# The bank of the gated rows' transposes in a mixture-of-experts block: from the two transpose banks to the six product banks

## The chip, the cores and the metric

The kernel runs on one core of one Trainium2 chip. The metric is the device time of one execution in microseconds (us); of several executions the median is taken.

## The reference, cut to what matters

A block of two layers works on 512 latent rows of 1024 numbers. Each layer has a token mixer and then a mixture of 32 SwiGLU experts, of which each row uses two; the change is in this second part, which runs once in each layer. Rows are sorted by expert and each expert's weights act on its own rows:

```
def expert_block(args):
    xi, e = args
    return (jax.nn.silu(xi @ w1[e]) * (xi @ w3[e])) @ w2[e]
...
y = jax.ops.segment_sum(yb * buf_w[:, None].astype(yb.dtype), buf_tok, num_segments=t + 1)
```

All 32 experts' weights are read in each layer, 6 MB an expert.

## The kernel before

**Pairs of experts.** The function `moe(l)` handles the experts of layer `l` in 16 pairs `p`. A pair has up to 64 rows for each of its two experts, side by side on 128 partitions; TensorE (PE) multiplies the two halves in two column halves of its array, with two sets of weights. A loop runs over pairs 0 to 14, and pair 15 is written out behind it. The whole function stands in a manual schedule: each engine gets its instructions in the order of the code.

**One pair on PE.** In order:

1. `gate_up` and `lin_up` (both line 1499): the rows times `w1` and times `w3`. ScalarE (ACT) takes the silu of the first, VectorE (DVE) multiplies the second with it (line 1508), which gives the gated rows `g`.
2. `scatter(*prev)` (lines 1562 and 1563): the rows of the pair before are added to their tokens by eight pairs of products with a selection matrix. DVE adds each of the eight results to `xs` (line 1564).
3. `turn_g(g)` (line 1514): four transposes of the gated rows into one bank `pg`, which ACT copies to `gT` (line 1516).
4. `turn` (line 1485): eight transposes of the next pair's input rows, four into each of two banks. DVE takes the first bank to `hT` with the modulation (line 1491), ACT the second (line 1489).
5. `down` (line 1526): `gT` times `w2` in two halves. DVE weighs them (line 1532), ACT and GpSimd split them for the next scatter.

**Banks.** PSUM, where PE writes, has eight banks; line 433 names them: two are `tr` (transposes) and six are `pj` (products). Each call of `bank` takes one of its kind that an earlier tile has used, and PE then waits until that tile's last reader is done with it.

**Branches.** An expert may have more than 64 rows. For that, three blocks under `tc.If(n > 64)` stand in each pair's code: behind `gate_up`, behind `lin_up`, and (lines 1644 to 1646) a whole `turn_g`, `down` and `scatter` between steps 2 and 3, which takes one `tr` and ten `pj` banks. The banks are laid out when the program is built, as if the blocks ran. In this execution two of the thirty blocks ran, and 28 were skipped. Where a block is skipped, each engine raises, in its place, the counts that the block would have raised, each after its own earlier work; whoever waits for a bank that the block used last waits for this raise. The same stands behind pair 15's scatter: a loop under an If (`rest`, line 1660) that was skipped in both layers.

**Weights.** They come in units of 2 MB into a ring of nine buffers, six units a pair, in the order in which they are used, through one DMA queue; a unit is asked for when its buffer comes free.

Of the kernel before, what the change touches and what calls it, by code (L numbers as in the profile page):

```python
# [34 lines left out]
class Net:  # L35
# [1424 lines left out]
    def moe(self, l):  # L1460
        tc, nc, I = self.tc, self.nc, self.I
        with ExitStack() as ms:
# [46 lines left out]

            def turn_g(g, gT=None):  # L1510

                pg = self.bank("tr")
                for k in range(4):
                    nc.tensor.transpose(pg[:, 128 * k:128 * k + 128], g[:, k::4], self.ident)  # L1514
                gT = wk.tile([128, 4, 128], F32, name="gT") if gT is None else gT[:, :512].rearrange("p (k d) -> p k d", k=4)
                nc.scalar.activation(gT, pg.rearrange("p (k d) -> p k d", k=4), AF.Copy)  # L1516
                return gT
# [67 lines left out]
            def block(p, c, g):  # L1585

                pool = self.rings["B"][0]
                ix = wk.tile([128, 1], I32, name="ix")
                iw = wk.tile([128, 2], F32, name="iw")
                nc.vector.tensor_copy(ix, self.gxc[:, bass.ds(c, 1)])  # L1590
                nc.vector.tensor_copy(iw[:, 0:1], self.tid[:, bass.ds(c, 1)])
                nc.vector.tensor_copy(iw[:, 1:2], self.wsl[:, bass.ds(c, 1)])
                hT = turn(gather(ix, hx[0]), hx[0])

                def unit(name, x):
                    w = pool.tile([128, 4096], F32, name="w")
                    nc.sync.dma_start(w, I[name][l, bass.ds(2 * p + x, 1)].rearrange("e (p k) n -> p (e k n)", p=128))
                    return w.rearrange("p (k n) -> p k n", n=1024 if name == "w2" else 512)
                gate_up(hT, (unit("w1", 0), unit("w1", 1)), g)
                lin_up(hT, (unit("w3", 0), unit("w3", 1)), g)  # L1600
                o = out()
                down(turn_g(g, hx[1]), (unit("w2", 0), unit("w2", 1)), iw[:, 0:1], iw[:, 1:2], o, g)
                scatter(*o)
# [20 lines left out]
            for p in range(15):  # L1624
                n = ns.pop(p)
                w = self.next_unit(), self.next_unit(1)
                g = wk.tile([128, 512], F32, name="g")
                gate_up(hT, w, g, () if p else (route, range(8)))
                with tc.If(n > 64):  # L1629

                    hTx = turn(hx[p % 2], hx[p % 2])
                    gate_up(hTx, w, gx)
                w = self.next_unit(), self.next_unit(1)
                lin_up(hT, w, g)
                with tc.If(n > 64):  # L1635
                    lin_up(hTx, w, gx)
                if p < 14:
                    hgs.append(gather(col(self.gix, p + 2), skip=True))
                    self.issue(self.taken)
                if prev:  # L1640
                    scatter(*prev)
                w = self.next_unit(), self.next_unit(1)
                prev = out()
                with tc.If(n > 64):
                    down(turn_g(gx, hx[p % 2]), w, col(self.tid, 16 + p), col(self.wsl, 16 + p), prev, gx)
                    scatter(*prev)
                gT = turn_g(g)
                hT = turn(hgs.pop(0))
                if p < 13:
                    ns[p + 2] = more(p + 2)  # L1650
                prev = out()
                down(gT, w, col(self.tid, p), col(self.wsl, p), prev, g, nc.gpsimd if p < 14 else nc.vector)
# [295 lines left out]
```

## Time and profile before

| | |
|---|---|
| median of 3 runs | 1859.27 us (1853.28 to 1860.14) |
| the profiled execution | 1858.2 us, its span 1856.1 us |
| mean granted clock of TensorE | 0.964 of 2.4 GHz |
| PE busy | 1682.1 us, 91% of the span |
| pairs of layer 0 | from about 620 us to about 1125 us |
| pairs of layer 1 | from about 1345 us to the end |

All times in the rows are us from the start of the span. PE rows are matmuls (a transpose is one), PEld rows the loads of the operand that stays in the array. "[1.97 <-DVEq L1660]" says that the engine sat idle for 1.97 us before the row, and what ended it; DVEq, PEq and SPq are the sequencers of these engines, which raise and wait for semaphores. A granted clock (PEclk) of 1.00 is 2.4 GHz and 0.50 is 1.2 GHz.

### The profile page before, as it was taken

To read this page: it belongs to the slowest core of one execution; us is meant where nothing else is said; L and a number is where in the kernel's file an instruction comes from. 1 tells how busy PE (TensorE), PEld (TensorE's weight loads), DVE (VectorE), ACT (ScalarE), POOL (GpSimd) and SP (SyncE) were. 2 spreads that over 40 slices of the span, in tenths; PEclk is the share of its full clock that TensorE was granted. 3 is DMA by queue.
4 is the path that set the end of the run, shared out by engine and by line. 5 is a ranking of instruction groups with operands and counts; after the bars stand their busy time and mean duration, and the time that the engine had idled before them with its cause. 6 is when DMAs were issued, how large, how long until landed. Compare 5 with 4: busy or idle time off the path is not lost. (4 is left out here: it accounts for less than half of the span.)

```text
span 1856.1 us, 26571 instructions
## 1 busy us (share of the span) xinstructions
PE 1682.1 (91%) x10229; PEld 1005.1 (54%) x10230; DVE 803.9 (43%) x1614; ACT 481.8 (26%) x888; POOL 419.4 (23%) x303
## 2 busy tenths in 40 slices
PE   5999988897989699999999998999789999999996
PEld 4766667766868244444344446688634444444442
DVE  5435778745773423323233237633523233323233
ACT  4466354522322111111111115233311111111012
POOL 1114465644510111011111103343111111111101
PEclk9999989998999799999999998999999999999998
DMA  9569985769944899999999864714589979999993
GB/s 328 199 231 338 283 224 171 173 162 257 228 163 158 343 424 427 425 424 426 425 425 424 367 257 148 278 45 181 227 320 425 427 294 427 426 424 426 426 425 150
DMA packets 154547, 572.27 MB, mean 308 GB/s; under 512 B 55208, under 2 KB 79961, under 8 KB 126214
## 3 DMA queue, kind: packets, MB, share of 16 engines
q1 hardware_dynamic: 148326, 555.26, 78.6%
q0 software_dynamic: 4896, 10.48, 1.5%
q10 hardware_dynamic: 1152, 4.19, 0.6%
q8 instruction: 112, 1.84, 0.4%
q14 instruction: 61, 0.50, 0.1%
HBM read 550.86 MB, written 26.38 MB: 311 GB/s over the span
## 5 line engine op out<-in xcount | busy, mean ns | idle before, releaser
L1499 PE MATMUL pj<-w,hT 128*64 128x512 f32 x2048 | 470.1, 597 | 16.8 <-DMA w<-in_w 10.4
L1499 PEld LDWEIGHTS pj<-w,hT 128*64 128x64 f32 x2048 | 171.1, 137 | 295.6 <-issue 259.5
L1526 PE MATMUL pj<-w,gT 128*64 128x512 f32 x960 | 212.6, 595 | 3.8 <-DVE hT L1491 2.6
L1537 POOL TENSOR_TENSOR ylo<-g,yhi 128x512 fp32r<-128x512 f32 x56 | 70.8, 1264 | 642.0 <-ACT yhi L1536 642.0
L1508 DVE TENSOR_TENSOR g<-pj,g 128x512 f32<-128x512 f32 x32 | 22.1, 692 | 435.7 <-PEq L1635 383.5
L1564 DVE TENSOR_TENSOR xs<-pj,xs 128x512 f32<-128x512 f32 x264 | 161.4, 681 | 4.7 <-PE pj L1563 0.9
L670 POOL TENSOR_TENSOR wlo<-w,whi 128x1024 fp32r<-128x1024 f32 x43 | 107.0, 2492 | 231.2 <-ACT whi L668 229.7
L1526 PEld LDWEIGHTS pj<-w,gT 128*64 128x64 f32 x960 | 77.2, 137 | 118.2 <-issue 111.9
L1532 DVE SCALAR_TENSOR_TENSOR g<-pj,wsl,gate 128x512 f32<-128x512 f32 x64 | 48.1, 751 | 174.4 <-PE pj L1526 154.2
L1516 ACT ACTIVATE gT<-tr 128x512 f32<-128x512 f32 x32 | 19.1, 597 | 371.7 <-PE tr L1514 371.7
L1562 PE MATMUL pj<-yhi,sel 128*128 128x512 f32 x264 | 106.7, 404 | 5.6 <-PEq L1635 2.4
L685 PE MATMUL pj<-w,whi 128*128 128x512 f32 x336 | 104.9, 392 | 0.6 <-ACT whi L668 0.6
L1563 PE MATMUL pj<-ylo,sel 128*128 128x512 f32 x264 | 103.5, 392 | 1.4 <-POOL ylo L1537 1.4
L685 PE MATMUL pj<-hhi,wlo 128*128 128x512 f32 x224 | 93.5, 417 | 10.0 <-POOL wlo L670 7.0
L685 PE MATMUL pj<-hhi,whi 128*128 128x512 f32 x224 | 93.1, 416 | 7.2 <-DVE cv L801 6.3
L685 PE MATMUL pj<-hlo,whi 128*128 128x512 f32 x224 | 91.2, 407 | 0.0
L1536 ACT ACTIVATE yhi<-g 128x512 fp32r<-128x512 f32 x62 | 39.0, 629 | 192.7 <-DVE g L1532 192.7
L1562 PEld LDWEIGHTS pj<-yhi,sel 128*128 128x128 f32 x264 | 49.5, 187 | 45.8 <-issue 32.5
L685 PEld LDWEIGHTS pj<-w,whi 128*128 128x128 f32 x336 | 63.6, 190 | 15.0 <-ACT whi L668 1.0
L668 ACT ACTIVATE whi<-w 128x1024 fp32r<-128x1024 f32 x53 | 55.2, 1052 | 55.8 <-PE pj L685 37.6
L1505 ACT ACTIVATE g<-pj 128x512 f32<-128x512 f32 x32 | 19.1, 597 | 185.4 <-PEq L1629 144.4
L685 PE MATMUL pj<-w,wlo 128*128 128x512 f32 x168 | 66.3, 394 | 0.0
(623 smaller groups left out, 2722.2 us busy)
## 6 DMA issues: line engine op xcount, KB each, us to landing
w<-in_w SPq DMA_DIRECT2D x188, 2048.0 KB
w<-in_ada_w SPq DMA_DIRECT2D x20, 2048.0 KB
w<-in_w_in_a SPq DMA_DIRECT2D x8, 2048.0 KB
w<-in_w_in_b SPq DMA_DIRECT2D x6, 2048.0 KB
w<-in_ada_w SPq DMA_DIRECT2D x8, 1024.0 KB
w<-in_w SPq DMA_DIRECT2D x8, 1024.0 KB
Y<-R SPq DMA_DIRECT2D x20, 256.0 KB
vp<-vscr SPq DMA_DIRECT2D x18, 256.0 KB
```

Of the source, the lines that this page charges most:

```text
L668: nc.scalar.activation(hi[:, :, :n], w, AF.Copy)
L670: (lo_eng or nc.gpsimd).tensor_tensor(lo[:, :, :n], w, hi[:, :, :n].bitcast(F32), op=OP.subtract)
L685: nc.tensor.matmul(out, n[j][0][:, k], n[j][1][:, k, a:b], start=(i == 0), stop=(i == 23))
L1499: nc.tensor.matmul(ps[64 * x:64 * x + 64], hT[:, k, 64 * x:64 * x + 64], w[x][:, k], start=(k == 0), stop=(k == 7))
L1508: nc.vector.tensor_tensor(g, up(hT, w, side), g, op=OP.mult)
L1526: nc.tensor.matmul(py[64 * x:64 * x + 64], gT[:, k, 64 * x:64 * x + 64], w[x][:, k, 512 * n:512 * n + 512], start=(k == 0), stop=(k == 3))
L1532: nc.vector.scalar_tensor_tensor(y, py, wi, self.gate[:, 512 * n:512 * n + 512], op0=OP.mult, op1=OP.mult)
L1536: nc.scalar.activation(o[0][:, c], y, AF.Copy)
L1537: eng.tensor_tensor(o[1][:, c], y, o[0][:, c].bitcast(F32), op=OP.subtract)
L1562: nc.tensor.matmul(ps, s, yhi[:, c], start=True, stop=False)
L1563: nc.tensor.matmul(ps, s, ylo[:, c], start=False, stop=True)
L1564: nc.vector.tensor_tensor(self.xs[:, t, c], ps, self.xs[:, t, c], op=OP.add)
```

## The change

`turn_g` takes its bank from the six of the products. Nothing else is edited. The call in the If block (line 1645) and the one in `rest` go through the same function, so they move too.

```
             def turn_g(g, gT=None):

-                pg = self.bank("tr")
+                pg = self.bank("pj")
                 for k in range(4):
                     nc.tensor.transpose(pg[:, 128 * k:128 * k + 128], g[:, k::4], self.ident)
                 gT = wk.tile([128, 4, 128], F32, name="gT") if gT is None else gT[:, :512].rearrange("p (k d) -> p k d", k=4)
```

## Rows read from the trace of the kernel before

**Rows 1.** The page: busy time, share and count of each engine.

```profile
PE 1682.1 (91%) x10229; PEld 1005.1 (54%) x10230; DVE 803.9 (43%) x1614; ACT 481.8 (26%) x888; POOL 419.4 (23%) x303
```

**Rows 2.** Busy time by stretches: start:end, length, engines, PEclk, DMA share, GB/s.

```profile
839.00:980.00 141.00, 129.80 (x573) 55.36 (x572) 40.64 (x75) 19.19 (x39) 18.64 (x16) 1.00 1.01 426
...
1706.00:1828.00 122.00, 113.03 (x501) 51.69 (x502) 38.57 (x70) 15.82 (x32) 9.58 (x8) 0.99 0.96 401
```

**Rows 3.** Timeline of one pair, layer 0, pair 2: start, length, engine, line.

```profile
697.03 4.87 DVE L1564 TENSOR_TENSOR xs<-pj,xs 128x512 f32<-128x512 f32 x8
...
699.74 0.39 PE L1563 MATMUL pj<-ylo,sel 128*128 128x512 f32 x1
700.25 0.56 PEld L1514 LDWEIGHTS tr<-ident,g 128*128 128x128 f32 x4 [0.54 <-issue]
...
700.72 0.54 PEld L1485 LDWEIGHTS tr<-ident,hg 128*128 128x128 f32 x4
...
701.04 0.60 ACT L1516 ACTIVATE gT<-tr 128x512 f32<-128x512 f32 x1 [11.50 <-PE tr L1514]
701.68 0.52 PEld L1485 LDWEIGHTS tr<-ident,hg 128*128 128x128 f32 x4 [0.43 <-ACT gT L1516]
...
702.05 1.37 DVE L1491 TENSOR_SCALAR hT<-tr,m 128x128 f32<-128x128 f32 x4 [0.15 <-DVEq L1644]
...
702.53 0.23 PEld L1526 LDWEIGHTS pj<-w,gT 128*64 128x64 f32 x4 [0.32 <-DVE hT L1491]
```

**Rows 4.** Instructions by line: who waited for line 1516 (us, times).

```profile
  PEld tr L1485: 13.0, 30
```

**Rows 5.** By line: line 1514's engine sat idle until (us, times).

```profile
  DVEq L1660: 3.9, 2
```

**Rows 6.** By line: the events of line 1644 on DVE's sequencer.

```profile
L1644 DVEq EVENT_SEMAPHORE x28: 21/21/21, 645.3 to 1797.8; - x28
```

**Rows 7.** Timeline of PE: starts of `turn_g` in both layers.

```profile
672.70 0.72 PE L1514 MATMUL tr<-ident,g 128*128 128x128 f32 x4
...
839.41 0.72 PE L1514 MATMUL tr<-ident,g 128*128 128x128 f32 x4
...
963.67 0.72 PE L1514 MATMUL tr<-ident,g 128*128 128x128 f32 x4
...
1074.74 0.72 PE L1514 MATMUL tr<-ident,g 128*128 128x128 f32 x4
...
1103.44 0.72 PE L1514 MATMUL tr<-ident,g 128*128 128x128 f32 x4 [1.97 <-DVEq L1660]
...
1540.09 0.72 PE L1514 MATMUL tr<-ident,g 128*128 128x128 f32 x4
...
1705.85 0.72 PE L1514 MATMUL tr<-ident,g 128*128 128x128 f32 x4 [0.15 <-PEq L1644]
...
1796.13 0.72 PE L1514 MATMUL tr<-ident,g 128*128 128x128 f32 x4 [0.15 <-PEq L1644]
...
1827.24 0.72 PE L1514 MATMUL tr<-ident,g 128*128 128x128 f32 x4 [1.90 <-DVEq L1660]
```

**Rows 8.** Stretches around long waits of PE, columns as in rows 2.

```profile
855.00:870.00 15.00, 12.68 (x52) 4.83 (x49) 2.22 (x4) 0.60 (x1) 0.00 (x0) 1.00 1.00 422
945.00:962.00 17.00, 14.39 (x61) 5.38 (x57) 2.26 (x4) 0.60 (x1) 0.03 (x1) 1.00 1.01 427
...
1725.00:1735.00 10.00, 9.37 (x33) 3.14 (x34) 0.63 (x1) 0.00 (x0) 0.00 (x0) 0.83 1.01 430
...
1098.00:1115.00 17.00, 15.03 (x56) 7.08 (x56) 7.04 (x12) 3.52 (x6) 0.00 (x0) 0.90 0.73 256
1822.00:1840.00 18.00, 16.11 (x59) 7.12 (x57) 6.97 (x12) 2.71 (x4) 0.00 (x0) 0.91 0.09 36
```

**Rows 9.** Timeline of PE: thirty matmuls of `lin_up` behind waits for weights.

```profile
860.44 7.08 PE L1499 MATMUL pj<-w,hT 128*64 128x512 f32 x30 [2.02 <-DMA w<-in_w]
...
1725.47 8.78 PE L1499 MATMUL pj<-w,hT 128*64 128x512 f32 x30 [1.71 <-DMA w<-in_w]
```

More of the change, by code (lines that the diff above doesn't have):

```diff
@@ L1510, in turn_g @@
             def turn_g(g, gT=None):
-                pg = self.bank("tr")
+                pg = self.bank("pj")
                 for k in range(4):
```

## The prediction

> **What bounds the kernel now.** I read the page first: PE is busy for 91% of the span [rows 1], so the question is which stretches have anything else behind them. The change touches the two stretches of expert pairs, so the busy time by stretches comes next [rows 2]: there PE and the DMA engines are both nearly full (DMA share 0.96 to 1.01). Which of the two sets the pace shows in the starts of `turn_g` on PE [rows 7]. In layer 0 the six pairs from 672.70 to 839.41 take 27.79 us each and the next four, to 963.67, take 31.07 us each, where the PE row shows waits for `w` [rows 9]. So PE leads at first, from a full ring, and the weights bind after that. Layer 1 goes the same way: 27.63 us each from 1540.09 to 1705.85, then 30.09 us.
>
> This gives the size of the cushion, PE's time lost to weights. Layer 0: 124.26 − 4 × 27.79 = 13.1 us. Layer 1: 90.28 − 3 × 27.63 = 7.4 us, and its last step, 31.11 us against 28.70 us in layer 0, 2.4 us more. Together 22.9 us. A PE that is slower ahead of such a wait meets its weights later and waits less; the loss counts only beyond this.
>
> **What the change removes.** With `pg` on `tr`, `turn`'s second bank is the one that `pg` just had, so its four transposes wait for ACT's copy of `gT`. The row shows 0.43 us [rows 3], and over the trace 13.0 us in 30 waits, 0.43 us each [rows 4]. With `pg` elsewhere `turn` has both its banks free. The gain is 0.43 us a pair; the copy itself is then covered: it ends 1.39 us behind the start of `pg` (701.04 + 0.60 − 700.25), and the twelve transposes that must go ahead of `down` take 0.56 + 0.54 + 0.52, about 1.6 us less the small overlap of the loads.
>
> **What it adds.** It moves `pg` to a bank that was last used inside the branch at line 1644. Every `pj` bank was: the block holds ten products and, now, one `pg`, in six banks. In 28 of 30 pairs the block is skipped [rows 6], and DVE's raise comes after its own earlier work, the eight adds. DVE's adds trail PE: eight take 4.87 us, from 697.03 to 701.90 [rows 3], while PE is done with the scatter at 700.13. `pg` now begins at 700.25, beside DVE's adds. With a `pj` bank it begins when DVE's raise has come: DVE's own next operation starts 0.15 us after the last add, behind that raise, at 702.05 [rows 3]. So PE stands for 702.05 − 700.25 = 1.80 us.
>
> The trace has this very wait twice already. Behind pair 15's scatter, `pg`'s bank was last used under the skipped `rest`, and PE stands for 1.97 and 1.90 us until DVE's raise [rows 5, 7]. That is the upper bound; the lower bound is 0, if the bank was released by an early add. I take 1.80 us, as it is worked out at the place itself and the two rows agree to 0.2 us.
>
> Net 1.80 − 0.43 = 1.37 us a pair. It applies to 30 pairs less the two that took the block (their banks wait for real adds that are long done) less the two first pairs, which have no scatter ahead and already wait for DVE: 26 pairs, 35.6 us. Pair 15 keeps its wait in both layers: no cost.
>
> What goes along with it: ACT's copy, `hT` on DVE (1.37 us) and ACT start 1.4 to 1.8 us later, and the next `gate_up` needs `hT` only behind the 32 matmuls of `down` (thirty of the kind take 7.08 us [rows 9]); without that cover each late us would be a us of PE. DVE has nothing more to do, so the adds do not move. Weights are asked for later by as much as PE is late, which is free while units wait in the queue (DMA share 0.96 to 1.01 [rows 2]). The next pair's products take their banks one step further round the six, behind the same raise or behind reads a whole step old: nothing.
>
> **The clock.** Long waits of PE cost twice when the clock falls behind them. Both of pair 15's waits are followed by a fall: the 17 us and the 18 us around them have a mean of 0.90 and 0.91 [rows 8], which is 3.4 us and 3.2 us at 1.2 GHz. Of the waits for weights, 1.71 us was followed by a fall (0.83 over 10 us, 3.4 us at the low level), but 2.02 us (at 860.44) and one within 945 to 962, where PE idles for 2.6 of 17 us, were not: both stretches are at 1.00 [rows 8, 9]. The price is in the thirty matmuls behind the waits: 8.78 us with the fall, 7.08 us without, 1.70 us [rows 9]. The bounds are none of the 26 waits (0) and all of them (44.2 us). The nearest rows are pair 15's, the same wait at the same place, two of two; the weights' waits fall less often. I take 20 of 26: 34.0 us.
>
> The Trainium skill's page "TensorE: Matmul & The Clock Gate", section "A second HAM failure mode: psum-queue depth-cycling", tells of a kernel that cycled through PSUM banks and idled so often between groups of matmuls that the clock kept going down and up, with throughput lost at each turn. The trace agrees for three waits and not for the two at 1.00. By that page every pair would pay, and the sum would be 12.7 + 44.2 = +56.9 us, 1915 us.
>
> **The sum.** 35.6 + 34.0 − 22.9 = +46.7 us. The profiled execution took 1858.2 us, 1.1 us under the median shown. 1858.2 + 46.7 = 1904.9, so about 1905 us.
>
> **The rivals.**
>
> *A, the clock mostly holds.* The same waits, with falls in 0 to 12 of 26. For it: the two stretches at 1.00 with waits as long. Against it: two of two at pair 15. None gives 35.6 − 22.9 = +12.7 us, 1871 us; twelve give 1891 us. Chance 0.28.
>
> *B, no wait at all: not slower.* The place is `pg`'s bank at line 1514. If PE needs only the add that read this one bank, then any of the first five adds is done (697.03 + 5 × 0.61 = 700.08) when `pg` begins at 700.25, and nothing is paid; from the sixth on the wait returns. Then only the 0.43 us is gained, and where the weights bind, the cushion eats it. It counts in layer 0 in the three pairs from 980 us on and in layer 1 in the first four, seven in all: −3.0 us, 1855 us. For it speaks how little of DVE's lag any one bank has; against it, that a skipped branch raises all its counts at once, behind the last add, and that this is what pair 15's wait shows. Chance 0.07.
>
> The Trainium skill's page "PSUM — Partial Sum Buffer", section "PSUM bank collisions raise a hardware error", gives the rule to guard PSUM with semaphores by bank and quadrant, thus against the engine that still uses that bank and no other. By that rule alone it would be B. Pair 15's waits, 1.97 and 1.90 us, are longer than one bank asks for.
>
> *C, the weights take it all.* If the net wait is under 22.9 / 26 = 0.88 us a pair and the clock holds, the PE that comes late finds its weights there and ends as before: about 1858 us. For it: 22.9 us of waits. Against it: 1.37 us by the rows. Chance 0.05.
>
> **How the numbers follow.** The forecast, falls in 13 or more pairs, has 0.60; its own range is 1893 to 1915 us (12.7 + 13 × 1.7 to 12.7 + 44.2). The whole range reaches down to A with no fall and a wait cheaper by 0.1 us (26 × 0.1 = 2.6), 1868, and up to all falls with half of the 0.17 us by which pair 15's wait is dearer (2.2), about 1918. It leaves out B and C. About 0.5% (9.3 us) is what a measurement of this kernel can tell from no change; B and C lie within it, and so does the cheap end of A: same 0.13, faster 0.02, slower 0.85.
>
> **What the profile will show.** Right: in 26 pairs the load for line 1514 idles about 1.8 us behind DVE's sequencer at line 1644; the idle time of line 1485 behind ACT's `gT` is gone; the starts of `turn_g` are about 29 us apart, or 30.7 us where the clock fell; waits for `w` on line 1499 are nearly gone; the mean granted clock is under 0.964 (20 falls of 3.4 us, half of it lost, is 34 us in 1905, so about 0.95). Wrong: a wait on line 1514 that is under 0.9 us says that the raise is not what it waits for (B or C); pairs 29 us apart with a clock as before say A; a second stretch at half clock behind one wait would push the time above the range.

## The result and the profile after

The change makes the kernel slower by 1.6%: 1887.8 us in the median against 1856.4 us for the kernel before, measured beside it, a ratio of 1.0159 (95% interval 1.0137 to 1.0180). The profiled execution took 1887.1 us, its span 1885.0 us, 28.9 us more than before's, at a mean granted clock of 0.953.

PE's busy time is all but the same as in [rows 1]; its share fell:

```profile
PE 1684.0 (89%) x10229; PEld 986.2 (52%) x10230; DVE 808.3 (43%) x1614; ACT 482.6 (26%) x888; POOL 417.1 (22%) x303
```

By line, what the loads of line 1514 stood idle for (us, times) in the trace after:

```profile
  DVEq L1644: 60.3, 26
  issue: 4.7, 2
  PEq L1644: 4.3, 2
```

In 26 pairs the load waits for DVE's sequencer at the skipped block. The time given there, 60.3 / 26 = 2.3 us, is the load unit's; PE itself, which still ends its last product, stands for 1.9 us. The 30 waits of line 1485 for ACT's `gT` [rows 4] are gone.

The timeline of PE, two pairs of layer 0 (start, length, engine, line):

```profile
791.82 0.75 PE L1514 MATMUL pj<-ident,g 128*128 128x128 f32 x4 [1.90 <-DVEq L1644]
792.40 1.06 PE L1485 MATMUL tr<-ident,hg 128*128 128x128 f32 x8
793.40 7.09 PE L1526 MATMUL pj<-w,gT 128*64 128x512 f32 x32
...
849.54 0.98 PE L1514 MATMUL pj<-ident,g 128*128 128x128 f32 x4 [1.88 <-DVEq L1644]
850.32 1.91 PE L1485 MATMUL tr<-ident,hg 128*128 128x128 f32 x8
852.16 7.62 PE L1526 MATMUL pj<-w,gT 128*64 128x512 f32 x32
```

Both pairs wait for 1.9 us. In the first the twelve transposes take 1.58 us until `down`, in the second 2.62 us: there the clock fell. The granted clock behind every such wait is in the windows of 27 us from each of the 26 starts (columns as in [rows 2]); three of the 26 stand here:

```profile
821.00:848.00 27.00, 26.20 (x124) 11.21 (x122) 7.40 (x14) 3.96 (x8) 3.53 (x3) 1.00 1.01 425
850.00:877.00 27.00, 26.54 (x119) 11.43 (x118) 5.96 (x12) 3.97 (x8) 3.54 (x3) 0.94 1.01 425
880.00:907.00 27.00, 26.54 (x118) 11.28 (x119) 5.48 (x11) 3.97 (x8) 3.54 (x3) 0.94 1.01 425
```

Nine windows are at 1.00 and seventeen at 0.94, eight in layer 0 and nine in layer 1 (0.06 × 27 × 2 = 3.2 us at 1.2 GHz). The two long stretches of [rows 2], 839 to 980 and 1706 to 1828, are now at 0.94 both.

The starts of `turn_g`: first, second, three neighbours, and pair 15 of layer 0; first and last of layer 1.

```profile
644.22 0.48 PE L1514 MATMUL pj<-ident,g 128*128 128x128 f32 x2 [1.30 <-DVEq L1644]
673.04 0.39 PE L1514 MATMUL pj<-ident,g 128*128 128x128 f32 x1 [1.88 <-DVEq L1644]
...
820.68 0.39 PE L1514 MATMUL pj<-ident,g 128*128 128x128 f32 x1 [1.92 <-DVEq L1644]
849.54 0.39 PE L1514 MATMUL pj<-ident,g 128*128 128x128 f32 x1 [1.88 <-DVEq L1644]
879.99 0.51 PE L1514 MATMUL pj<-ident,g 128*128 128x128 f32 x2 [1.89 <-DVEq L1644]
...
1115.37 0.36 PE L1514 MATMUL pj<-ident,g 128*128 128x128 f32 x1 [1.96 <-DVEq L1660]
1384.99 0.39 PE L1514 MATMUL pj<-ident,g 128*128 128x128 f32 x2 [1.46 <-DVEq L1644]
...
1857.86 0.36 PE L1514 MATMUL pj<-ident,g 128*128 128x128 f32 x1 [1.94 <-DVEq L1660]
```

In the trace of before, whose last starts are in [rows 7], the layers begin here:

```profile
645.07 0.48 PE L1514 MATMUL tr<-ident,g 128*128 128x128 f32 x2 [0.95 <-DVEq L1635]
...
1373.28 0.48 PE L1514 MATMUL tr<-ident,g 128*128 128x128 f32 x2 [0.95 <-DVEq L1635]
```

A pair takes 28.86 us without a fall (849.54 − 820.68) and 30.45 us with one (879.99 − 849.54): a fall costs 1.6 us. Before, a step in which no wait for weights shows takes 27.58 us (672.70 to 700.28 on PE). From the first `turn_g` to the last, layer 0 takes 471.15 us (before: 1103.44 − 645.07 = 458.37) and layer 1 472.87 us (before: 453.96): 31.7 us more. The end behind the last `turn_g` is 1.7 us shorter (27.14 against 28.86 us), since the clock does not fall right behind it (1.00 from 1858 to 1866 us, where before had 0.87 from 1827 to 1840); what lies ahead of layer 0 and between the layers is 1.1 us shorter. 31.7 − 1.7 − 1.1 = 28.9.

Waits for weights are gone. What line 1499 stood idle for, after (us, times; loads and matmuls together):

```profile
  issue: 258.1, 944
  PEq L1629: 40.2, 56
  DVEq L1629: 7.5, 26
  DVE hx L1491: 3.0, 6
  DVE g L1532: 1.2, 4
  PE pj L1499: 1.1, 4
  DVE hT L1491: 0.8, 2
  DVE g L1508: 0.6, 2
```

No row says `DMA w`, where the loads alone had this before:

```profile
  DMA w<-in_w: 19.3, 12
```

### The profile page after: what moved, and what is told of

Read it like the earlier page. It is cut to its first block, busy times and chain, and to the rows that moved or that the text cites. A ratio compares the mean times of both kernels' runs of the same rounds, so it can differ in the third digit from the quotient of the medians.

```text
span 1885.0 us, 26574 instructions
## 1 busy us (share of the span) xinstructions
PE 1684.0 (89%) x10229; PEld 986.2 (52%) x10230; DVE 808.3 (43%) x1614; ACT 482.6 (26%) x888; POOL 417.1 (22%) x303
## 5 line engine op out<-in xcount | busy, mean ns | idle before, releaser
L1499 PE MATMUL pj<-w,hT 128*64 128x512 f32 x2048 | 455.9, 595 | 9.0 <-PEq L1629 8.9
L1499 PEld LDWEIGHTS pj<-w,hT 128*64 128x64 f32 x2048 | 157.6, 137 | 288.0 <-issue 242.1
L1526 PE MATMUL pj<-w,gT 128*64 128x512 f32 x960 | 232.5, 640 | 0.0
L1526 PEld LDWEIGHTS pj<-w,gT 128*64 128x64 f32 x960 | 70.8, 149 | 142.0 <-issue 139.6
L1516 ACT ACTIVATE gT<-pj 128x512 f32<-128x512 f32 x32 | 19.1, 597 | 401.5 <-PE pj L1514 401.5
L1514 PE MATMUL pj<-ident,g 128*128 128x128 f32 x128 | 24.1, 312 | 56.0 <-DVEq L1644 52.1
L1562 PEld LDWEIGHTS pj<-yhi,sel 128*128 128x128 f32 x264 | 49.5, 187 | 45.8 <-issue 32.5
```

The costliest lines, as they stand in the source:

```text
L1499: nc.tensor.matmul(ps[64 * x:64 * x + 64], hT[:, k, 64 * x:64 * x + 64], w[x][:, k], start=(k == 0), stop=(k == 7))
L1526: nc.tensor.matmul(py[64 * x:64 * x + 64], gT[:, k, 64 * x:64 * x + 64], w[x][:, k, 512 * n:512 * n + 512], start=(k == 0), stop=(k == 3))
L1562: nc.tensor.matmul(ps, s, yhi[:, c], start=True, stop=False)
```

## The experiments

The theory: the whole loss is the raise of a skipped block, which DVE makes behind its eight adds, and the falls of the clock that follow such waits. The rivals: a product bank costs in itself (DVE's adds trail PE), or eleven banks a block in six are too many.

**Which of the two calls matters.** The first kernel gives only the main call a product bank, the second only the call in the block (and in `rest`).

```
-                pg = self.bank("pj")
+                pg = self.bank("pj" if gT is None else "tr")     # first
+                pg = self.bank("tr" if gT is None else "pj")     # second
```

> The kernel after, but only the turn_g of every pair (the main call) has its bank among the six of the products; the call in the skipped If block (and in rest) has its bank from the two for transposes again. Theory 'raise': the main pg still gets a bank that the scatter inside the If block used last, so it waits for DVE's raise behind the eight adds as in the kernel after: about 1.9 us idle at line 1514 in 26 pairs, 16 to 18 falls of the clock, 1883 to 1893 us. Rival 'crowding' (eleven banks a block in six is what costs): with ten in the block and the wait gone or shorter, 1858 to 1872 us.

Measured: 1893.2 us, ratio to before 1.0168 (1.0141 to 1.0194). Line 1514's loads:

```profile
  DVEq L1644: 60.2, 26
```

> The kernel after, but the main turn_g has its bank from the two for transposes again; only the call in the skipped If block keeps its bank among the six of the products. Theory 'raise': no wait at line 1514 outside pair 15, the 0.43 us wait of turn's second bank for ACT's copy is back, and the time is that of the kernel before, 1853 to 1862 us. Rival 'crowding': the block still holds eleven product banks, so a good part of the 31 us stays, over 1870 us.

Measured: 1857.5 us, ratio 0.9988 (0.9974 to 1.0002): the kernel before. The main call carries all of it; a crowded block costs nothing. The profiled execution of the first kernel has a span of 1897.3 us, and by the same windows, the clock fell in 22 of the 26 pairs instead of 17. Five falls are 8 of the 12.3 us between the two spans, so the waits, which are alike, do not set the number of falls. The kernel after varies by itself too: its six executions took 1881.6 to 1895.1 us, the slowest at the lowest clock (0.949).

**A bank of its own.**

```
-            self.banks = {"tr": 2, "pj": 6}
+            self.banks = {"tr": 2, "pj": 5, "pg": 1}
...
-                pg = self.bank("pj")
+                pg = self.bank("pg")
...
-        self.acc = [self.bank("pj") for _ in range(2)]
+        self.acc = [self.bank("pj"), self.bank("pg")]
```

> The kernel after, but pg has a bank of its own (two for transposes, five for products, one for pg); the two accumulators at the end of layer 0 take one of each kind so that all eight banks are still used there. The last user of pg's bank is then the skipped block's ACT copy, so PE waits for ACT's raise, and ACT is done long before. Theory 'raise': no idle time behind DVE's sequencer at line 1514 in the 26 pairs, the 0.43 us behind ACT's copy is gone as well, the clock holds as in the kernel before, 1848 to 1858 us. Rival 'any bank other than the two for transposes costs' or 'too few product banks': with five product banks it is slower still than after, 1885 us or more.

Measured: 1866.8 us, ratio 1.0049 (1.0031 to 1.0067): above what the theory gave and below what the rival gave. The trace tells why. Line 1514's loads wait for no other engine, and the pairs are quicker than before, 775.38 − 748.03 = 27.35 us:

```profile
748.03 0.48 PE L1514 MATMUL pg<-ident,g 128*128 128x128 f32 x2 [0.30 <-PEq L1644]
775.38 0.48 PE L1514 MATMUL pg<-ident,g 128*128 128x128 f32 x2 [0.30 <-PEq L1644]
...
1095.63 0.48 PE L1514 MATMUL pg<-ident,g 128*128 128x128 f32 x2 [0.51 <-PEq L1660]
1371.21 0.48 PE L1514 MATMUL pg<-ident,g 128*128 128x128 f32 x2 [0.95 <-DVEq L1635]
```

But from pair 15 of layer 0 to the first pair of layer 1 it takes 275.6 us, where before took 1373.28 − 1103.44 = 269.8 us: the mixer there has five banks instead of six. Behind the last `turn_g`, at 1824.00 us, it takes 32.5 us, where before took 28.9 us, and PE stands there three times for 0.8 us until DVE has added (before: once for 0.7 us). Neither was in the expectation. The two losses, 5.8 and 3.6 us, less the 2.6 us that the layers win, come to 6.8 us, near the 7.6 us between the medians. (The profiled execution, 1858.6 us, is the quickest of the four; its pairs began 6.4 us earlier than before's.) A later kernel lends it the bank back (the last experiment).

**The clock, with the wait kept.** PE gets work in the place where it stood.

```
+                if p:
+                    pf = self.bank("tr")
+                    for _ in range(2):
+                        nc.tensor.matmul(pf[:, :448], self.ident, self.tok[:, :448], start=True, stop=True)
                 gT = turn_g(g)
```

> The kernel after, with two extra matmuls (128x448 each, into a bank for transposes, never read) between the skipped If block and turn_g in every pair but the first: PE works where it stood idle. They change no output. Theory 'the clock is half of the loss': pg still begins when DVE's raise has come, so the waits' own 1.1 to 1.3 us a pair stays, but the clock no longer falls behind it: under 4 falls in the pairs, about 1.6 us less in each of 17 pairs, 27 us less, some of which the weights take back, so 1858 to 1872 us. Rival 'the wait alone is the loss, the clock falls anyway or costs nothing because the weights bind': 1883 to 1893 us.

Measured: 1869.2 us, ratio 1.0048 (1.0031 to 1.0064). In the timeline of PE the extra matmuls (line 1650, two rows each) end as `turn_g` begins:

```profile
786.04 1.74 PE L1650 MATMUL tr<-tok,ident 128*128 128x448 f32 x4
787.77 0.74 PE L1514 MATMUL pj<-ident,g 128*128 128x128 f32 x4
...
816.48 0.39 PE L1514 MATMUL pj<-ident,g 128*128 128x128 f32 x1
```

A pair takes 28.71 us (816.48 − 787.77), 0.15 us less than after without a fall, and the clock fell behind none of the 26 waits; its one fall among the pairs, at 954 us, stands behind a wait for weights. So 18.6 us of the 31.4 went with the falls, if not by them alone: 17 × 1.6 = 27.2, and 26 × 0.15 = 3.9 which this kernel lacks elsewhere (below), less some 12 us that the weights take back (most of it in the steps at 903 and 933 us, 30.2 and 35.5 us).

**The wait split in two.** `turn` stands ahead of `turn_g`.

```
-                gT = turn_g(g)
                 hT = turn(hgs.pop(0))
+                gT = turn_g(g)
```

> The kernel after with the two calls swapped: turn (eight transposes of the next pair's rows, into the two transpose banks) stands ahead of turn_g. The DVE raise that pg waits for is then about half covered by turn's eight transposes (about 1.1 us), and ACT's copy gT comes later, with 0.5 to 1 us of PE idle ahead of down. Theory 'raise, and the clock falls behind long waits': the wait is split in two short ones with work between them, so the path is about as long as in the kernel after without its falls, fewer than 8 falls, 1858 to 1875 us. Rival 'the clock falls as long as the sum of the idle time is the same': 1883 to 1893 us.

Measured: 1866.4 us, ratio 1.0042 (1.0022 to 1.0062). PE still stands idle, but in two pieces, 0.60 and 0.74 us:

```profile
786.81 1.14 PE L1485 MATMUL tr<-ident,hg 128*128 128x128 f32 x8
788.54 0.75 PE L1514 MATMUL pj<-ident,g 128*128 128x128 f32 x4 [0.60 <-DVEq L1644]
790.03 2.79 PE L1526 MATMUL pj<-w,gT 128*64 128x512 f32 x12 [0.74 <-ACT gT L1516]
...
817.32 0.39 PE L1514 MATMUL pj<-ident,g 128*128 128x128 f32 x1 [0.60 <-DVEq L1644]
```

The step is 28.78 us, and again no fall follows these waits (the one fall among the pairs, at 953 us, stands behind a wait of 2.41 us for weights). All in all PE stands idle for nearly as long as after, 87.00 − 80.41 = 6.6 us in some three pairs here (first row) against 28.90 − 26.50 = 2.4 us in one pair after (second row):

```profile
788.00:875.00 87.00, 80.41 (x372) 34.89 (x372) 26.93 (x49) 12.05 (x26) 10.61 (x9) 1.00 1.01 425
...
791.80:820.70 28.90, 26.50 (x125) 11.55 (x125) 8.83 (x16) 3.97 (x8) 3.55 (x3) 1.00 1.01 425
```

So it is the one long wait that the falls follow, and not the sum of the idle time.

**No block.** Lines 1644 to 1646 are left out of both kernels, and with them the rows beyond 64 of two pairs.

```
-                with tc.If(n > 64):
-                    down(turn_g(gx, hx[p % 2]), w, col(self.tid, 16 + p), col(self.wsl, 16 + p), prev, gx)
-                    scatter(*prev)
```

> The kernel before without the third If block (lines 1644 to 1646): the rows beyond 64 of two pairs of experts are left out of the result, which takes their work out of the time as well (about 23 us in each of the two pairs by their longer step in the trace, 46 us). It is the measure for its partner, the same edit of the kernel after. Both theories: 1805 to 1825 us, unless the block's events cost time themselves.

> The kernel after without the third If block (the rows beyond 64 of two pairs are left out, as in its partner): pg has a bank of the six of the products, but no skipped block has used it last; it is one that an early add of the same pair's scatter has read. Theory 'raise': without a raise behind all eight adds pg need not wait, or only for one add that is long done: no idle time over 0.3 us at line 1514 in the pairs, and the time is within 6 us of its partner, or below it by up to 10 us (0.43 us a pair less). Rival 'a bank of the products costs in itself, since DVE's adds trail PE': idle time of 1 us or more at line 1514 in all pairs and 20 to 31 us over its partner.

Measured: 1827.8 us without the change and 1826.3 us with it; the ratios to before are 0.9826 (0.9801 to 0.9851) and 0.9817 (0.9794 to 0.9841). The first came out 3 us over its range: I had counted 23 us for each taken block, from the longer step of its pair, but that step also holds the work of the other two blocks, which stay in. In the trace of before the third block of layer 0 lasts from 1006.74 to 1019.82 us on PE, 13.1 us, and the step of its pair is 12.8 us shorter without it (43.39 against 56.15). The pair of them decides what was asked. With a product bank whose last reader is an add of the same scatter, and no block:

```profile
700.26 0.51 PE L1514 MATMUL pj<-ident,g 128*128 128x128 f32 x3
726.81 0.39 PE L1514 MATMUL pj<-ident,g 128*128 128x128 f32 x2
```

No wait, 26.55 us a pair. Its partner, with a transpose bank:

```profile
732.42 0.39 PE L1514 MATMUL tr<-ident,g 128*128 128x128 f32 x2
759.62 0.39 PE L1514 MATMUL tr<-ident,g 128*128 128x128 f32 x2
```

27.20 us. A product bank is no burden; under the skipped block's raise it is. And 0.6 us less in each pair shows nothing in the time: the loads' waits for `w` grow from 27.2 us in 15 to 36.8 us in 19:

```profile
  DMA w<-in_w: 36.8, 19
```

**The own bank, shared.** As the own bank above, with pg's bank lent out where the pairs don't run:

```
-                py = self.bank("pj")
+                py = self.bank(("pj", "pg")[n])
...
-                    p = self.bank("pj")
+                    p = self.bank("pj" if i % 6 else "pg")
...
-                    ps = self.bank("pj")
+                    ps = self.bank(("pj", "pg")[t % 2])
```

> The kernel with pg in a bank of its own (two for transposes, five for products, one for pg), which the stages outside the pairs share: down_half's second half, every sixth product of the mixer and every second of its output products take pg's bank, so they have six again. In the pairs it is as with the own bank alone: no wait for DVE at line 1514, 27.3 us a pair where the weights don't bind, 0.25 us less than before. Theory 'the own bank lost outside the pairs, and the weights take what the pairs gain': the stretch from the last turn_g of layer 0 to the first of layer 1 is back from 275.6 us to 270 us, and the time is 1852 to 1861 us, no more than 0.5% from the kernel before on either side. Rival 'five product banks cost inside the pairs': the time stays at 1864 to 1870 us. Rival 'the pairs' gain counts in full': 26 x 0.25 = 6.5 us under before, 1846 to 1852 us.

Measured: 1854.4 us, ratio 0.9978 (0.9967 to 0.9989), 0.2% under before.

```profile
752.77 0.48 PE L1514 MATMUL pg<-ident,g 128*128 128x128 f32 x2 [0.30 <-PEq L1644]
780.10 0.48 PE L1514 MATMUL pg<-ident,g 128*128 128x128 f32 x2 [0.30 <-PEq L1644]
...
1099.99 0.48 PE L1514 MATMUL pg<-ident,g 128*128 128x128 f32 x2 [0.45 <-PEq L1660]
1369.79 0.48 PE L1514 MATMUL pg<-ident,g 128*128 128x128 f32 x2 [0.94 <-DVEq L1635]
```

Between the layers it takes 269.8 us again, and behind the last `turn_g` 29.7 us, so the five banks had cost there. This version keeps what the change was good for, turns `pg` loose from the raise, and is quicker than both kernels, than before by about half of the 6.5 us that the pairs save (26 × 0.25): in the layers the profiled execution keeps 2.8 us of them, and the loads' waits for `w` are 23.6 us instead of 19.3.

## Why the prediction was right in its direction and too high in its size

The chain held: a bank last used in the skipped block, a raise behind eight adds, a wait of PE, falls of the clock behind it, weights that give part back. It gave +46.7 us; the profiled execution shows +28.9. Term by term:

| term | predicted | measured (weights: what is left) |
|---|---|---|
| 26 pairs, wait less gain | 1.37 each, 35.6 | 1.28 each, 33.3 |
| falls | 20 × 1.70 = 34.0 | 17 × 1.6 = 27.2 |
| weights | −22.9 | 33.3 + 27.2 − 31.7 = 28.8 back |
| outside the layers | 0 | −2.8 |

**The wait** was right: 1.75 us (a gap of 1.90 us before `turn_g` where before had 0.15), against 1.80. Experiments one, two, three and the pair without the block show that it is the raise and nothing else about the bank.

**The gain** was too small: from `turn_g` to `down` it now takes 1.57 to 1.58 us instead of 2.18 (pair 1) to 2.38 (pair 3), at least 0.6 us and not 0.43. The 0.32 us that the loads of `down` stood idle ahead of their first matmul [rows 3] shrank as well; the row was there and I did not count it.

**A cost that I put at nothing** stands at the skipped first block, where `lin_up` begins. In the timeline of PE, before:

```profile
744.46 7.09 PE L1499 MATMUL pj<-w,hT 128*64 128x512 f32 x32 [0.16 <-PEq L1629]
```

and after:

```profile
749.93 7.09 PE L1499 MATMUL pj<-w,hT 128*64 128x512 f32 x32 [0.31 <-PEq L1629]
```

0.15 us in nearly every pair: 1.75 − 0.61 + 0.15 = 1.29, the step's 1.28 us. This is the term that the prediction called "nothing", the next products' banks one step further round. The queue of the loads shows what goes with it, a second semaphore event on line 1499 in nearly every pair, before and after:

```profile
L1499 PEldq EVENT_SEMAPHORE  x37: 51/51/51, 623.9 to 1800.8; - x37
L1499 PEldq EVENT_SEMAPHORE  x68: 51/51/51, 623.4 to 1840.7; - x68
```

Every kernel with the gap of 0.3 us has 64 or 68 of these events (the own banks, the first kernel, `turn` ahead), and every kernel with 0.15 us has 37 to 41 (the second kernel, the extra matmuls, both without the block). So the 0.15 us goes with one more semaphore event ahead of the loads. Why the kernel with the extra matmuls, which takes its product banks in the order of after, is spared it stays open.

**The clock** is the largest miss, with the weights. Pair 15's two falls of two made me take 20 of 26; it was 17 here and 22 in the first kernel above with the same waits. That falls come behind these waits, and are worth about what the thirty matmuls said [rows 9], 1.6 against 1.70 us, was right; how many was a guess between bounds, and the runs show that no single number is to be had. The case that I forecast (13 or more) came true; its own range, 1893 to 1915 us, did not hold the median of 1887.8, since the other terms were high.

The Trainium skill's page "TensorE: Matmul & The Clock Gate", section "A second HAM failure mode: psum-queue depth-cycling", tells of a clock that goes down and up where PE idles between groups as its banks come round, and this trace agrees in kind (17 falls behind bank waits). That every pair would pay was my reading, for the page gives no count, and nine of the 26 waits were followed by no fall.

**The weights** took back 28.8 us and not 22.9, by what is left of the sum. I had counted the steps that were plainly long. Of the steps of 27.7 to 28.3 us some held small waits for weights too (0.45 us of a load at 828 us), in others `down` began 0.1 to 0.2 us later than in pair 1, and the fall behind a wait for weights at 1725 us [rows 9] went with them. That the weights, more than PE, set the time of the kernel before is borne out from the other side by the pair without the block, where 0.65 us less in each pair left the time as it was.

**Rival B**, no wait at all, is the kernel after without the block: there one early add is what PE needs, and the wait is nil. The Trainium skill's page "PSUM — Partial Sum Buffer", section "PSUM bank collisions raise a hardware error", asks for a guard by bank and quadrant; that trace agrees with it, and the kernel after shows that a skipped branch asks for more than the bank does.

**The end of layer 1** was not in the sum: pair 15's wait is as long as before (1.94 against 1.90 us [rows 7]), but no fall follows it in this execution, 1.7 us.

## What to carry to other kernels

When buffers are shared between straight code and a branch that is nearly always skipped, ask who used the buffer last in the program as built: the skipped branch's raise comes behind all earlier work of the engine that makes it, so a buffer that was free long ago is late by that engine's whole lag (here 1.9 us of DVE's). Give the code on the critical path a buffer whose last user in the branch is an engine that is early, and lend it out where the branch is not near. Before pricing a shorter step, look at what the next bound takes of it: here some 29 of 60 us lost, and half or all of what two other versions gained, went to the weights.

## What the hardware showed that I had not expected

Equal waits were not followed by equal clocks. PE stood for 1.88 to 1.92 us in each of the 26 pairs, yet the windows are at 0.94 for five pairs in a row in layer 0 (from 850 us) and for six in layer 1 (from 1676 us), and at 1.00 for three in a row just ahead of each. In a run of falls each pair is as long as the last, 30.5 us. Two pieces of 0.60 and 0.74 us, with eight transposes before and four between, brought no fall behind them in any pair. What sets a run off is not settled here.
